# Gathered attention biases, key and query parts written straight to their partitions, 8 weight buffers, norm chunks one group ahead, 55 activation tiles

## Chip, cores and metric

The kernel runs on one core of a Trainium2 chip. The metric is the device time of one execution in microseconds (us), taken as the median of several runs; lower is better. TensorE (PE) does the matmuls, VectorE (DVE), ScalarE (ACT) and GpSimd (POOL) the elementwise work, and SyncE (SP) issues the DMAs.

## What is computed

Two layers of a diffusion backbone over 256 latent and 256 context tokens of width 1024. Cut to what matters:

```python
for l in range(2):
    h, hc = ffn_half_step(h, ...ffn1), ffn_half_step(hc, ...ffn1)
    u, uc = modulate(rmsnorm(h, g_mix)), modulate(rmsnorm(hc, g_mix))
    nq, nk, nv, fu, wq, wk, wv, gl = split_projection(u @ w_in[l])      # context likewise
    a = neighbourhood_attention(nq, nk, nv, nk_c, nv_c, na_bias[l])     # 8 heads of 64
    f = fourier_mix(fu)
    w = window_gqa_attention(rope(wq), rope(wk), wv, wk_c, wv_c, sink)  # 8 query heads, 2 key heads
    h = h + gt2 * merge_branches(a, f, w, gl, w_br[l], w_out[l])
    h = ffn_half_step(h, ...ffn2)                # the context stream stops after layer 0
return rmsnorm(h, g_final)
```

`ffn_half_step` is RMSNorm, scale and shift, SwiGLU of inner width 2816, and a gated addition to `h`. In the neighbourhood attention a latent query of column c sees 16 columns around c in all four grid rows, with a bias from a table of 15 by 31 entries for each head, and all context keys.

## The kernel before

Activations lie feature by token: a tile `act` (or `tmp`) is 128 partitions by 512 tokens in fp32, and 66 such tiles form one pool (`N_ACT`). Every product is done in three matmuls (`mm3`, lines 286 to 291): a value x is split into a rounded part "hi" and a remainder "lo" (= x - hi), and hi*hi, hi*lo and lo*hi are added up in PSUM. So each weight tile and each activation is split by one ACT instruction (hi) and one subtraction (lo).

The order of the instructions is written out by hand (`manual_schedule`): each engine runs its instructions in the order in which the program emits them, and waits in that order. A tile taken from a pool whose previous holder still has readers makes the first writer wait for the last of them.

Weights (`Weights`, lines 43 to 100) come as 424 sub-tiles of 128x1024 (8 tiles of 128x128). SP loads them into `raw` (line 58), ACT writes `wh` (line 67), DVE writes `wl` (line 76; POOL during attention and in the first FFN's first groups). `wh` and `wl` share the pool `w` of 6 buffers. At the first tile of sub-tile n (`next`, line 90) the program emits `wh` up to sub-tile n+2, and at its middle `wl` up to n+2.

A norm (`Norm`) makes the input u of a stage in 16 steps: step t (`_step`, lines 196 to 215) scales one 128x256 piece of `h` on DVE (line 206), adds the shift on ACT and rounds (line 208), and the piece of step t-1 gets its "lo" on DVE (line 214). `chunks(k)` runs the steps up to t = k+1. In an FFN the function `first` (lines 521 to 545) calls it ahead of the matmuls of group k: 4 weight tiles of 12 matmuls on 256 columns, first for the 8 latent pieces, then for the 8 context pieces. Two groups use one sub-tile of weights.

The mixer (`mix`, lines 844 to 1055): the Fourier branch and values are projected first, then `attention` (lines 713 to 842) walks over blocks (head pair p, latent or context queries) in a software pipeline: scores on PE (lines 726 and 727), mask and maximum on DVE (line 733), exp on ACT (line 735), normalising on DVE (line 752), transposes on PE (line 757), the split of the transposed weights on ACT (line 759) and DVE (line 764), and values on PE (line 775). Between its steps `fill` emits pieces of the projections of later blocks by due times. When a projection is done, `plain` (line 886, neighbourhood heads) or `rope` (line 896, window heads) takes it out of PSUM. `rope` turns it first: 4 small DMAs (line 903) and 3 POOL operations (line 906). Both then write hi (ACT, lines 889 and 909) and lo (DVE, lines 891 and 911) as 128-partition tiles, and `stack` (line 870) builds the operands of the scores from them by DMA on SP (line 884): for a query two tiles holding [hi0; lo0] and [lo1; hi1] of the two heads on 64 partitions each (4 DMAs), for a key four tiles [hi0; hi0], [hi1; hi1], [lo0; lo0], [lo1; lo1] (8 DMAs). There are 5 keys and 8 queries in each layer. Layer 0 works on 512 query tokens, layer 1 on 256; keys have 512 in both.

The masks of the neighbourhood attention: `mix_loads` takes 8 tiles `nab` from the activation pool in each layer, clears their context half on POOL (line 444) and loads the first head pair; `na_bias_load` (line 694) issues 8 DMAs for each head pair, which read rows of 64 fp32 numbers from a padded table, and `na_bias` (line 711) adds a window mask on POOL, 4 operations for each head pair. `bias_ahead` (line 1003) does that for the next pair in mid-attention and issues the loads of the pair after it.

Of the kernel before, what the change touches and what calls it, by code (L numbers as in the profile page):

```python
# [27 lines left out]
BIAS_W = 2 * GRID_W - 1  # L28
# [6 lines left out]
N_ACT = 66  # L35
# [224 lines left out]
class Emit:  # L260
    def __init__(self, ctx, tc, d):
        self.tc, self.nc, self.d = tc, tc.nc, d
        pool = lambda name, bufs, **k: ctx.enter_context(tc.tile_pool(name=name, bufs=bufs, **k))
        self.const = pool("const", 1)
        self.act_p = pool("act", N_ACT)
        self.raw_p = pool("raw", 5)
        self.w_p = pool("w", 6)
        self.mod_p = pool("mod", 2)
        self.sm_p = pool("sm", 4)
        self.ps_p = pool("ps", 8, space=PSUM)  # L270
        self.W = Weights(self.nc, d["ws"], self.raw_p, self.w_p)
        self.mod = {}
# [90 lines left out]
    def setup(self):  # L363
# [56 lines left out]
        self.na_mask = c.tile([128, NLAT], F32, name="na_mask")  # L420
# [5 lines left out]
    def setup_mix(self):  # L426
        nc, d = self.nc, self.d
        nc.sync.dma_start(out=self.g_fin, in_=d["g_final"])
        nc.sync.dma_start(out=self.cos, in_=d["cos"])
        nc.sync.dma_start(out=self.sin, in_=d["sin"])  # L430
        nc.sync.dma_start(out=self.na_mask, in_=d["na_mask"])
        nc.sync.dma_start(out=self.wa_mask, in_=d["wa_mask"])
        nc.sync.dma_start(out=self.sink, in_=d["sink"].partition_broadcast(128))
        yield
        nc.gpsimd.tensor_scalar(out=self.nsink, in0=self.sink, scalar1=-1.0, scalar2=None, op0=ALU.mult)

    def mix_loads(self, l):

        self.raw_dft = [self.tmp() for _ in range(2)]
        self.nc.sync.dma_start(out=self.raw_dft[0], in_=self.d["dft_n"])  # L440
        self.nc.sync.dma_start(out=self.raw_dft[1][:, :256], in_=self.d["dft_d"])
        self.nab = [[self.tmp() for _ in range(4)] for _ in range(2)]
        for t in self.nab[0] + self.nab[1]:
            self.nc.gpsimd.memset(t[:, NLAT:], 0.0)  # L444
        self.na_bias_load(l, 0)

# [61 lines left out]
    def ffn(self, l, which, n, norm, nxt):  # L508
# [12 lines left out]
        def first(passes):  # L521
# [3 lines left out]
            for vs in passes:  # L525
                lo, hi = 256 * vs[0], 256 * (vs[-1] + 1)
                for k in range(KD):
                    norm.chunks(vs[0] * KD + k)
# [165 lines left out]
    def na_bias_load(self, l, p):  # L694


        nc = self.nc
        tab = self.d["na_bias"]
        for i in range(4):
            t4 = self.nab[p % 2][i][:, :NLAT].rearrange("p (r c) -> p r c", c=GRID_W)  # L700
            hp, qt = divmod(i, 2)
            for r2 in range(2):
                first = WIN_R - 1 - (2 * qt + r2)
                off = ((l * 8 + 2 * p + hp) * GRID_W * (2 * WIN_R - 1) + first) * BIAS_W + GRID_W - 1
                src = bass.AP(tensor=tab.tensor, offset=tab.offset + off,
                              ap=[[(2 * WIN_R - 1) * BIAS_W - 1, GRID_W], [BIAS_W, ROWS], [1, GRID_W]])
                nc.sync.dma_start(out=t4[r2 * 64:r2 * 64 + 64], in_=src)  # L707

    def na_bias(self, p):
        for t in self.nab[p % 2]:  # L710
            self.nc.gpsimd.tensor_tensor(out=t[:, :NLAT], in0=t[:, :NLAT], in1=self.na_mask, op=ALU.add)
# [132 lines left out]
    def mix(self, l, norm, nxt):  # L844
# [9 lines left out]
        self.na_bias(0)  # L854
        self.na_bias_load(l, 1)
# [14 lines left out]
        def stack(name, hi, lo, n):  # L870


            a, b = self.act(), self.act()
            x, y = slice(0, 64), slice(64, 128)
            if "q" in name[0]:
                moves = (a, x, hi, x), (a, y, lo, x), (b, x, lo, y), (b, y, hi, y)
                res[name] = a, b
            else:
                c, d = self.act(), self.act()
                moves = ((a, x, hi, x), (a, y, hi, x), (b, x, hi, y), (b, y, hi, y),  # L880
                         (c, x, lo, x), (c, y, lo, x), (d, x, lo, y), (d, y, lo, y))
                res[name] = a, b, c, d
            for t, i, s, j in moves:
                nc.sync.dma_start(out=t[i, :n].bitcast(F32), in_=s[j, :n].bitcast(F32))

        def plain(scale):
            def evac(name, ps, n):
                hi, lo = self.act(), self.act()
                nc.scalar.activation(out=hi[:, :n], in_=ps[:, :n], func=AF.Copy, scale=scale)
                yield  # L890
                nc.vector.scalar_tensor_tensor(out=lo[:, :n], in0=ps[:, :n], scalar=scale,
                                               in1=hi[:, :n].bitcast(F32), op0=ALU.mult, op1=ALU.subtract)
                stack(name, hi, lo, n)
            return evac

        def rope(scale):
            def evac(name, ps, n):
# [10 lines left out]
                hi, lo = self.act(), self.act()  # L908
                nc.scalar.activation(out=hi[:, :n], in_=t, func=AF.Copy, scale=scale)
                yield  # L910
                nc.vector.scalar_tensor_tensor(out=lo[:, :n], in0=t, scalar=scale, in1=hi[:, :n].bitcast(F32),
                                               op0=ALU.mult, op1=ALU.subtract)
                stack(name, hi, lo, n)
# [89 lines left out]
        def bias_ahead(p):  # L1003
            self.na_bias(p)
            if p < 3:
                self.na_bias_load(l, p + 1)

# [122 lines left out]
def constants():  # L1130
# [7 lines left out]
    c = np.arange(GRID_W)  # L1138
    start = np.clip(c - WIN_C // 2, 0, GRID_W - WIN_C)
    inside = (c[None] >= start[:, None]) & (c[None] < start[:, None] + WIN_C)  # L1140
    na = np.where(inside, 0.0, NEG).astype(f)
# [13 lines left out]
        "na_mask": np.tile(na, (2, ROWS)),  # L1155
# [6 lines left out]
def pack(inputs, order):  # L1162
# [13 lines left out]
    pad = GRID_W - WIN_C  # L1176
    t = np.pad(w["na_bias"], ((0, 0), (0, 0), (0, 0), (pad, pad)))
    a["na_bias"] = np.broadcast_to(t[:, :, None], t.shape[:2] + (GRID_W,) + t.shape[2:])
# [31 lines left out]
    "na_bias": (DEPTH, 8, GRID_W, 2 * WIN_R - 1, BIAS_W), "sink": (DEPTH, 4, 4), "ident": (128, 128),  # L1210
    "cos": (128, NLAT), "sin": (128, NLAT), "na_mask": (128, NLAT), "wa_mask": (128, 2, NT),
# [18 lines left out]
```

## Time and profile before

| | us |
|---|---|
| median of 3 runs | 2122.66 (2122.08 to 2125.06) |
| profiled execution, its own time | 2120.81 |
| its span, first to last instruction | 2119.0 |
| PE busy / share of span | 2050.9 / 97% |
| DVE busy / share | 1283.7 / 61% |
| ACT busy / share | 848.5 / 40% |
| POOL busy / share | 355.7 / 17% |

The profiled execution is one run of the same program with the profiler on; its time stands 1.85 us below the median of the plain runs and 1.8 us above its own span. A stage can be found in the trace by its lines: the span runs through the first FFN of layer 0 (0 to 420 us), its mixer (420 to 860), second FFN (860 to 1240), and the same three of layer 1 (from 1240, 1600 and 1905).

### The profile page before, as it was taken

What the parts mean: (1) busy time and instruction counts of PE and PEld (TensorE: products, weight loads), DVE (VectorE), ACT (ScalarE), POOL (GpSimd) and SP (SyncE); (2) the same over time, 40 slices, a digit from 0 to 9 for tenths busy, and PEclk for the clock granted to TensorE, in tenths of its full rate; (3) what the DMA queues carried; (4) which work ended last, traced back from release to release, by engine and by line L of the source; (5) the groups of instructions that cost most, each with busy time, mean ns of one, the idle gap of its engine ahead of it and who ended that gap; (6) DMA issues with size and microseconds to landing.
All of it is one profiled execution on the core that took longest, in us unless ns stands there. A gap on an engine that the chain in (4) does not pass through costs nothing. (4 is left out here: it accounts for less than half of the span.)

```text
span 2119.0 us, 29168 instructions
## 1 busy us (share of the span) xinstructions
PE 2050.9 (97%) x11193; PEld 1764.7 (83%) x11193; DVE 1283.7 (61%) x2035; ACT 848.5 (40%) x1362; POOL 355.7 (17%) x285
## 2 busy tenths in 40 slices
PE   7899999999999999999999989999999989999998
PEld 3688888878888888988888788888888878999998
DVE  6777776566675334687777465533336548566554
ACT  4422222345786222432222243222324458545443
POOL 4200000403441112300000220000012155330002
PEclk9999999999999999999999999999999999999999
DMA  7465566455532333466666545623344563554663
GB/s 271 139 199 182 196 199 212 124 152 144 136 85 73 100 92 98 150 186 193 199 189 200 186 143 186 199 90 100 99 112 145 145 177 110 160 179 153 186 181 109
DMA packets 119412, 327.05 MB, mean 154 GB/s; under 512 B 30692, under 2 KB 35940, under 8 KB 119272
## 3 DMA queue, kind: packets, MB, share of 16 engines
q1 hardware_dynamic: 119272, 325.18, 50.3%
q8 instruction: 88, 1.44, 0.3%
q14 instruction: 52, 0.43, 0.1%
HBM read 305.99 MB, written 1.05 MB: 145 GB/s over the span
## 5 line engine op out<-in xcount | busy, mean ns | idle before, releaser
L290 PE MATMUL ps<-act,wh 128*128 128x512 f32 (+1 forms) x3227 | 1120.9, 347 | 24.1 <-DVE act L229 13.6
L289 PE MATMUL ps<-act,wh 128*128 128x512 f32 (+1 forms) x3227 | 1121.3, 347 | 3.4 <-ACT act L298 1.9
L291 PE MATMUL ps<-act,wl 128*128 128x512 f32 (+1 forms) x3227 | 1118.9, 347 | 1.8 <-DVE wl L76 1.8
L67 ACT ACTIVATE wh<-raw 128x1024 fp32r<-128x1024 f32 x424 | 447.4, 1056 | 707.8 <-PE ps L290 573.7
L290 PEld LDWEIGHTS ps<-act,wh 128*128 128x128 f32 x3227 | 613.2, 190 | 101.8 <-DVE act L229 14.8
L289 PEld LDWEIGHTS ps<-act,wh 128*128 128x128 f32 x3227 | 613.1, 190 | 78.9 <-ACT act L298 2.5
L291 PEld LDWEIGHTS ps<-act,wl 128*128 128x128 f32 x3227 | 613.1, 190 | 77.9 <-DVE wl L76 2.9
L76 DVE TENSOR_TENSOR wl<-raw,wh 128x1024 fp32r<-128x1024 f32 x379 | 474.6, 1254 | 273.6 <-ACT wh L67 273.0
L311 DVE CUSTOM_DVE_ANT_0 dump<-ada,silu_row 128x1024 bf16<-128x1024 f32 x224 | 273.3, 1220 | 13.9 <-DMA ada<-in_w_ada 11.5
L298 ACT ACTIVATE act<-tmp 128x512 fp32r<-128x512 f32 (+1 forms) x122 | 66.9, 566 | 275.2 <-DVE tmp L516 261.8
L471 DVE SCALAR_TENSOR_TENSOR h<-ps,mod,h 128x256 f32<-128x256 f32 x136 | 61.7, 480 | 150.8 <-PE ps L291 150.8
L76 POOL TENSOR_TENSOR wl<-raw,wh 128x1024 fp32r<-128x1024 f32 x45 | 110.7, 2461 | 222.9 <-ACT wh L67 199.7
L454 POOL TENSOR_TENSOR tmp<-h 128x512 f32<-128x512 f32 (+1 forms) x7 | 11.6, 1661 | 782.3 <-DVE h L471 639.8
L516 DVE TENSOR_TENSOR tmp<-tmp,ps 128x512 f32<-128x512 f32 (+1 forms) x88 | 54.6, 621 | 112.1 <-PE ps L291 107.5
L299 DVE TENSOR_TENSOR act<-tmp,act 128x512 fp32r<-128x512 f32 (+1 forms) x122 | 74.3, 625 | 62.2 <-ACT act L298 62.2
L764 DVE TENSOR_TENSOR act<-ps,act 128x512 fp32r<-128x512 f32 x80 | 54.8, 685 | 35.8 <-ACT act L759 27.6
L735 ACT ACTIVATE tmp<-tmp,sm 128x512 f32<-128x512 f32 (+1 forms) x96 | 62.2, 648 | 32.8 <-DVE sm L733 31.5
L775 PE MATMUL ps<-act 128*128 128x256 f32 x320 | 63.0, 309 | 12.4 <-DVE act L764 11.2
L460 POOL TENSOR_TENSOR tmp<-h 128x256 f32<-128x256 f32 (+1 forms) x44 | 51.7, 1174 | 117.8 <-DVE h L471 112.9
L759 ACT ACTIVATE act<-ps 128x512 fp32r<-128x512 f32 x80 | 47.5, 593 | 39.9 <-PE ps L757 34.5
L444 POOL MEMSET tmp<- 128x256 f32 x16 | 4.8, 312 | 348.6 <-PE ps L291 347.9
L775 PEld LDWEIGHTS ps<-act 128*128 128x128 f32 x320 | 44.8, 189 | 17.5 <-DVE act L764 15.0
(110 smaller groups left out, 1372.8 us busy)
## 6 DMA issues: line engine op xcount, KB each, us to landing
raw<-in_ws SPq DMA_DIRECT2D x424, 512.0 KB, 3.7
ada<-in_w_ada SPq DMA_DIRECT2D x128, 512.0 KB, 3.9
act<-act SPq DMA_DIRECT2D x112, 128.0 KB, 2.3
tmp<-in_w_ada_sc SPq DMA_DIRECT2D x16, 256.0 KB, 5.2
tmp<-in_w_ada SPq DMA_DIRECT2D x16, 256.0 KB, 6.0
tmp<-in_na_bias SPq DMA_DIRECT2D x64, 64.0 KB, 2.7
h<-in_h SPq DMA_DIRECT2D x8, 256.0 KB, 5.2
act<-act SPq DMA_DIRECT2D x32, 64.0 KB, 2.0
```

The costliest lines, as they stand in the source:

```text
L67: self.nc.scalar.activation(out=wh, in_=self.raw[i], func=AF.Copy)
L76: self.lo_engine.tensor_tensor(out=wl, in0=self.raw.pop(i), in1=self.hi[i].bitcast(F32), op=ALU.subtract)
L289: mm(ps, lhsT=w[0], rhs=x[0], start=start, stop=False)
L290: mm(ps, lhsT=w[0], rhs=x[1], start=False, stop=False)
L291: mm(ps, lhsT=w[1], rhs=x[0], start=False, stop=stop)
L298: nc.scalar.activation(out=hi, in_=src, func=AF.Copy)
L299: nc.vector.tensor_tensor(out=lo, in0=src, in1=hi.bitcast(F32), op=ALU.subtract)
L311: self.nc.vector.tensor_tensor_reduce(out=self.dump[:, ks], in0=w, in1=self.silu_row[:, v, ks], scale=1.0, scalar=m if half else 0.0, op0= ...
L471: self.nc.vector.scalar_tensor_tensor(out=h, in0=ps, scalar=self.mod[l, g][:, v, j:j + 1], in1=h, op0=ALU.mult, op1=ALU.add)
L735: nc.scalar.activation(out=e[:, :nk], in_=e[:, :nk], func=AF.Exp, scale=-1.0, bias=nm, accum_out=b["sum"][:, i:i + 1])
L764: nc.vector.tensor_tensor(out=t[1], in0=ps, in1=t[0].bitcast(F32), op=ALU.subtract)
L775: nc.tensor.matmul(b["ps"][hp][:, :256], lhsT=v, rhs=t[j][:, cs], start=c == 0 and j == 0, stop=c == n - 1 and j == 1)
```

## The change

- `na_bias` is prepared outside the program as full 256x256 masked tables, so that one DMA of 512 KB loads a head pair; the POOL additions, the mask tile and its load are gone. `nab` becomes two tiles of 128 x 4 x 512 for the whole run, cleared once in `setup`, and both are loaded in `mix_loads`.
- `stack` reads the projection itself and writes the parts to the partitions where they belong: two ACT and two DVE instructions on 64 partitions each. A query needs no DMA any more, a key 4. The 128-partition hi and lo tiles are gone.
- The `w` pool has 8 buffers; `ahead` is as it was.
- In `first`, `chunks` is called for one group further (not in the very first FFN).
- `N_ACT` is 55.

```diff
-N_ACT = 66
+N_ACT = 55
-        self.w_p = pool("w", 6)
+        self.w_p = pool("w", 8)
@@ setup
-        self.na_mask = c.tile([128, NLAT], F32, name="na_mask")
+        self.nab = [c.tile([128, 4, NT], F32, name=f"nab{i}") for i in range(2)]
+        for t in self.nab:
+            nc.gpsimd.memset(t[:, :, NLAT:], 0.0)
@@ mix_loads
-        self.nab = [[self.tmp() for _ in range(4)] for _ in range(2)]
-        for t in self.nab[0] + self.nab[1]:
-            self.nc.gpsimd.memset(t[:, NLAT:], 0.0)
         self.na_bias_load(l, 0)
+        self.na_bias_load(l, 1)
@@ ffn, first
-                    norm.chunks(vs[0] * KD + k)
+                    norm.chunks(vs[0] * KD + k + (not norm.ready))
@@ na_bias_load (its loops of 8 DMAs, and na_bias, are gone)
+        self.nc.sync.dma_start(out=self.nab[p % 2][:, :, :NLAT], in_=self.d["na_bias"][l, p])
@@ mix
-        self.na_bias(0)
-        self.na_bias_load(l, 1)
-        def stack(name, hi, lo, n):
-            a, b = self.act(), self.act()
+        def stack(name, src, scale, n):
             x, y = slice(0, 64), slice(64, 128)
+            a, b = self.act()[:, :n], self.act()[:, :n]
             if "q" in name[0]:
-                moves = (a, x, hi, x), (a, y, lo, x), (b, x, lo, y), (b, y, hi, y)
+                parts = (a, x, a, y, x), (b, y, b, x, y)
+                moves = ()
             else:
-                c, d = self.act(), self.act()
-                moves = ((a, x, hi, x), (a, y, hi, x), (b, x, hi, y), (b, y, hi, y),
-                         (c, x, lo, x), (c, y, lo, x), (d, x, lo, y), (d, y, lo, y))
-            for t, i, s, j in moves:
-                nc.sync.dma_start(out=t[i, :n].bitcast(F32), in_=s[j, :n].bitcast(F32))
+                c, d = self.act()[:, :n], self.act()[:, :n]
+                parts = (a, x, c, x, x), (b, y, d, y, y)
+                moves = (a, x, y), (b, y, x), (c, x, y), (d, y, x)
+            for hi, i, _, _, s in parts:
+                nc.scalar.activation(out=hi[i], in_=src[s], func=AF.Copy, scale=scale)
+            yield
+            for hi, i, lo, j, s in parts:
+                nc.vector.scalar_tensor_tensor(out=lo[j], in0=src[s], scalar=scale, in1=hi[i].bitcast(F32),
+                                               op0=ALU.mult, op1=ALU.subtract)
+            for t, i, j in moves:
+                nc.sync.dma_start(out=t[j].bitcast(F32), in_=t[i].bitcast(F32))
+            res[name] = (a, b) if "q" in name[0] else (a, b, c, d)
@@ plain and rope: both now end in stack(name, ps or t, scale, n)
@@ na_block
-                            after=(lambda: bias_ahead(p + 1)) if lat and p < 3 else None,
-                            mask=self.nab[p % 2] if lat else [zero] * 4,
+                            after=(lambda: self.na_bias_load(l, p + 2)) if lat and p < 2 else None,
+                            mask=[self.nab[p % 2][:, i, :] for i in range(4)] if lat else [zero] * 4,
```

## Rows read from the trace of the kernel before

**Rows 1.** The page, busy us, share of the span and instructions of each engine

```profile
PE 2050.9 (97%) x11193; PEld 1764.7 (83%) x11193; DVE 1283.7 (61%) x2035; ACT 848.5 (40%) x1362; POOL 355.7 (17%) x285
```

**Rows 2.** Stretches: length, busy PE, PEld, DVE, ACT, POOL, PE clock, DMA share, GB/s

```profile
500.00:680.00 180.00, 174.78 (x971) 147.99 (x970) 124.13 (x308) 134.12 (x325) 73.57 (x60) 1.00 0.41 109
1240.00:1280.00 40.00, 32.26 (x246) 30.34 (x245) 26.38 (x46) 19.64 (x30) 1.23 (x2) 1.00 0.44 134
1600.00:1640.00 40.00, 37.44 (x239) 33.32 (x238) 28.78 (x51) 21.05 (x33) 8.48 (x11) 1.00 0.55 159
1660.00:1820.00 160.00, 146.36 (x1017) 133.96 (x1016) 91.94 (x189) 104.24 (x226) 79.02 (x56) 0.99 0.54 143
```

**Rows 3.** ACT, then DVE, in time, start of layer 1's first FFN

```profile
1254.17 1.06 ACT L67 ACTIVATE wh<-raw 128x1024 fp32r<-128x1024 f32 x1 [1.09 <-PE ps L290]
1258.52 1.06 ACT L67 ACTIVATE wh<-raw 128x1024 fp32r<-128x1024 f32 x1 [1.09 <-PE ps L290]
...
1255.27 1.22 DVE L76 TENSOR_TENSOR wl<-raw,wh 128x1024 fp32r<-128x1024 f32 x1 [1.55 <-ACT wh L67]
1257.59 0.47 DVE L214 SCALAR_TENSOR_TENSOR act<-tmp,mod,act 128x256 fp32r<-128x256 f32 x1
```

**Rows 4.** ACT in time, start of layer 0's second FFN

```profile
884.61 1.06 ACT L67 ACTIVATE wh<-raw 128x1024 fp32r<-128x1024 f32 x1
887.78 1.04 ACT L67 ACTIVATE wh<-raw 128x1024 fp32r<-128x1024 f32 x1
```

**Rows 5.** Waits of the whole span: who, for whom, us, times, longest

```profile
PE ps L290 <- DVE act L214: 7.5, 6, 1.4
```

**Rows 6.** Waits, 1660 to 1820 us, PE and ACT

```profile
PE ps L775 <- DVE act L764: 9.0, 7, 2.9
...
ACT wh L67 <- PE ps L290: 16.0, 8, 4.4
```

**Rows 7.** Waits, 1698 to 1728 us

```profile
DVE act L891 <- DMA act<-act: 7.5, 1, 7.5
DVE act L764 <- DMA act<-act: 7.4, 1, 7.4
...
PE ps L932 <- ACT tmp L928: 2.2, 1, 2.2
...
PE ps L757 <- ACT tmp L900: 1.4, 1, 1.4
```

**Rows 8.** SP in time, 1698 to 1717 us: start, us, instructions merged

```profile
1697.46 5.33 SPq L707 DMA_DIRECT2D tmp<-in_na_bias  x8
1706.67 7.82 SPq L884 DMA_DIRECT2D act<-act  x12
```

**Rows 9.** By line: duration ns min/median/max, first and last start, forms

```profile
L891 DVE SCALAR_TENSOR_TENSOR act<-ps,act x16: 411/684/693, 478.0 to 1707.6; 128x512 fp32r<-128x512 f32 x12, 128x256 fp32r<-128x256 f32 x4
L911 DVE SCALAR_TENSOR_TENSOR act<-tmp,act x10: 462/692/2126, 569.6 to 1773.5; 128x512 fp32r<-128x512 f32 x6, 128x256 fp32r<-128x256 f32 x4
L889 ACT ACTIVATE act<-ps x16: 364/578/600, 477.3 to 1700.8; 128x512 fp32r<-128x512 f32 x12, 128x256 fp32r<-128x256 f32 x4
L781 ACT ACTIVATE tmp<-ps x96: 361/379/387, 523.1 to 1814.0; 64x256 f32<-64x256 f32 x96
```

**Rows 10.** Waits of PE, 500 to 680 us

```profile
PE ps L726 <- DMA act<-act: 1.8, 1, 1.8
```

**Rows 11.** DVE in time at the start of layer 1's mixer

```profile
1614.82 0.83 DVE L214 SCALAR_TENSOR_TENSOR act<-tmp,mod,act 128x256 fp32r<-128x256 f32 x1 [0.19 <-ACT act L208]
1618.22 2.88 DVE L76 TENSOR_TENSOR wl<-raw,wh 128x1024 fp32r<-128x1024 f32 x2
```

**Rows 12.** Memsets by line (as rows 9); POOL and ACT in time at the start

```profile
L444 POOL MEMSET tmp<- x16: 312/312/313, 232.2 to 1433.3; 128x256 f32 x16
...
26.59 3.38 POOL L221 TENSOR_TENSOR tmp<-h,tmp 128x512 f32<-128x512 f32 x2
...
30.09 1.09 ACT L227 ACTIVATE act<-tmp,mod,mod 128x256 fp32r<-128x256 f32 x2 [4.00 <-DVE mod L318]
```

More of the change, by code (lines that the diff above doesn't have):

```diff
@@ L27 @@
 WINDOW = 128
-BIAS_W = 2 * GRID_W - 1
 O_NA_Q, O_NA_K, O_NA_V, O_FN, O_WA_Q, O_WA_K, O_WA_V, O_GATE = (
@@ L430, in setup_mix @@
         nc.sync.dma_start(out=self.sin, in_=d["sin"])
-        nc.sync.dma_start(out=self.na_mask, in_=d["na_mask"])
         nc.sync.dma_start(out=self.wa_mask, in_=d["wa_mask"])
@@ L694, in na_bias_load @@
     def na_bias_load(self, l, p):
[L697 to L711, printed above, removed]
+        self.nc.sync.dma_start(out=self.nab[p % 2][:, :, :NLAT], in_=self.d["na_bias"][l, p])
     def attention(self, makers, fill):
@@ L868, in project @@
                 yield
-        def stack(name, hi, lo, n):
-            a, b = self.act(), self.act()
+        def stack(name, src, scale, n):
             x, y = slice(0, 64), slice(64, 128)
+            a, b = self.act()[:, :n], self.act()[:, :n]
             if "q" in name[0]:
-                moves = (a, x, hi, x), (a, y, lo, x), (b, x, lo, y), (b, y, hi, y)
-                res[name] = a, b
-            else:
-                c, d = self.act(), self.act()
-                moves = ((a, x, hi, x), (a, y, hi, x), (b, x, hi, y), (b, y, hi, y),
-                         (c, x, lo, x), (c, y, lo, x), (d, x, lo, y), (d, y, lo, y))
-                res[name] = a, b, c, d
-            for t, i, s, j in moves:
-                nc.sync.dma_start(out=t[i, :n].bitcast(F32), in_=s[j, :n].bitcast(F32))
-        def plain(scale):
[L887 to L894, printed above, removed]
+                parts = (a, x, a, y, x), (b, y, b, x, y)
+                moves = ()
+            else:
+                c, d = self.act()[:, :n], self.act()[:, :n]
[10 more added lines that the diff above has]
+            res[name] = (a, b) if "q" in name[0] else (a, b, c, d)
+        def plain(scale):
+            return lambda name, ps, n: stack(name, ps[:, :n], scale, n)
         def rope(scale):
@@ L907, in evac @@
                 yield 1
[L908 to L913, printed above, removed]
+                yield from stack(name, t, scale, n)
             return evac
@@ L1001, in mix @@
         zero = self.wa_mask[:, 0, NLAT:]
[L1003 to L1006, printed above, removed]
         def split_out(o, p):
@@ L1137, in constants @@
     cos, sin = np.cos(ang).T, np.sin(ang).T
[L1138 to L1141, printed above, removed]
     band = np.where(np.abs(t[:, None] - t[None]) <= WINDOW, 0.0, NEG).astype(f).reshape(2, 128, NLAT)
@@ L1154, in constants @@
         "sin": np.concatenate([-sin, sin] * 2, 0),
-        "na_mask": np.tile(na, (2, ROWS)),
         "wa_mask": wa,
@@ L1175, in pack @@
     a["w_ada_sc"] = w["w_ada"][0, :, D:2 * D].reshape(KD, 128, 2, 512).transpose(2, 0, 1, 3)
-    pad = GRID_W - WIN_C
-    t = np.pad(w["na_bias"], ((0, 0), (0, 0), (0, 0), (pad, pad)))
-    a["na_bias"] = np.broadcast_to(t[:, :, None], t.shape[:2] + (GRID_W,) + t.shape[2:])
+    c, t = np.arange(GRID_W), np.arange(NLAT)
+    start = np.clip(c - WIN_C // 2, 0, GRID_W - WIN_C)
+    inside = (c[None] >= start[:, None]) & (c[None] < start[:, None] + WIN_C)
+    row, col = t // GRID_W, t % GRID_W
+    dr = row[None] - row[:, None] + WIN_R - 1
+    dc = np.clip(col[None] - col[:, None], 1 - WIN_C, WIN_C - 1) + WIN_C - 1
+    b = np.full((DEPTH, 8, NLAT, NLAT), NEG, np.float32)
+    inside = np.tile(inside, (ROWS, ROWS))
+    b[:, :, inside] = w["na_bias"][:, :, dr[inside], dc[inside]]
+    a["na_bias"] = b.reshape(DEPTH, 4, 2, 2, 128, NLAT).transpose(0, 1, 4, 2, 3, 5).reshape(DEPTH, 4, 128, 4, NLAT)
     s = w["wa_sink"]
@@ L1209 @@
     "c": (128, KD, 2), "b_ada": (128, DEPTH, 9, KD), "gains": (128, DEPTH, 3, 8), "g_final": (128, 8),
-    "na_bias": (DEPTH, 8, GRID_W, 2 * WIN_R - 1, BIAS_W), "sink": (DEPTH, 4, 4), "ident": (128, 128),
-    "cos": (128, NLAT), "sin": (128, NLAT), "na_mask": (128, NLAT), "wa_mask": (128, 2, NT),
+    "na_bias": (DEPTH, 4, 128, 4, NLAT), "sink": (DEPTH, 4, 4), "ident": (128, 128),
+    "cos": (128, NLAT), "sin": (128, NLAT), "wa_mask": (128, 2, NT),
     "dft_n": (128, 2 * NLAT), "dft_d": (128, 256),
```

## The prediction

> **What bounds the kernel now.** I read the page first: PE is busy for 97% of the span [rows 1], so an engine with less work helps only where PE waits for it. No matmul is added, taken away or reordered here, so the whole effect must come out of PE's idle time, some 68 us (2119.0 less 2050.9). The first 80 us, where much of that lies, are touched only by two memsets. I then read the table of stretches for idle time elsewhere: 7.7 us at the start of layer 1's first FFN (40 less 32.26), 5.2 us in layer 0's attention, 2.6 us where layer 1's mixer starts, and 13.6 us in layer 1's attention, the largest [rows 2]. Last I read, for those stretches, who ended the waits, and the instructions in order of time.
>
> At the FFN start PE waits six times, 7.5 us in all, for the "lo" part of a norm chunk, DVE L214 [rows 5]. The time order shows a loop: ACT's conversion `wh` waits 1.09 us for PE to leave a weight buffer, DVE's `wl` waits for that `wh`, and the chunk that PE needs next stands behind `wl` on DVE; one turn takes 1258.52 - 1254.17 = 4.35 us [rows 3]. The same work in layer 0's second FFN, where ACT does not wait for PE, turns in 887.78 - 884.61 = 3.17 us [rows 4].
>
> In layer 1's attention the largest waits of PE (2.9, 2.2 and 1.4 us) lie within 12 us of each other [rows 6, 7]. Just ahead DVE stood 7.5 and 7.4 us until a DMA `act<-act` had read a tile: the pool gave its slot to a new writer, and the move that still had to read the old hi or lo tile was queued on SP [rows 7]. SP was busy with 8 bias loads (5.33 us) and 12 moves in a row (7.82 us) [rows 8]. So the bound there is SP's issue time, through the tile pool.
>
> **The change part by part.** The sum is made against the profiled execution (2120.81 us); the median of the runs shown, 2122.66, is 1.85 us higher, and I carry the difference over to it.
>
> (1) 8 weight buffers and chunks one group ahead. The buffers take away ACT's wait for PE, the earlier chunk takes L214 out of the group that needs it; either cuts the loop. I take the turn of rows 4 for that of rows 3: 6 waits x 1.18 us = 7.1 us gained. Next late is DVE and ACT's own rhythm, which is why the turn stays at 3.17. Bounds: 3.5 us if only half of the turns shorten, 8.5 us if the group in hand also covers some of that rhythm in both FFNs. The chunk's DVE and ACT instructions only move; what they pass on DVE is one `wl` (1.22 us, rows 3), which has a sub-tile in hand.
>
> (2) The bias loads become one DMA instead of 8 for each head pair, queries lose their 4 moves and keys 4 of 8: in the stretch of rows 8 seven of the eight bias issues and more than half of the moves go, some 9 of 13 us. The hi and lo tiles whose slots DVE waited for exist no more. I count the three waits of PE (2.9 + 2.2 + 1.4) as gone: 6.5 us. Bounds: 3.5 us (half), 13.6 us (all idle time of the stretch).
>
> (3) Against that each of the 26 stacks gets one more ACT and one more DVE instruction. That a half of the partitions is no cheaper is shown by L781, 379 ns on 64 partitions against 364 for the same 256 columns on 128 [rows 9]. So a stack costs up to 0.58 us more on ACT and 0.69 on DVE (512 columns), 0.36 and 0.41 to 0.46 on 256. All of DVE's would be 13 x 0.69 in layer 0 and 5 x 0.69 + 8 x 0.44 in layer 1, 16.0 us. PE does wait for DVE there: 9.0 us in 7 times for L764 [rows 6], of which 2.9 belong to (2), the rest mostly where L764 stands behind L911. I charge layer 1's five window stacks in full (0.69 + 4 x 0.46 = 2.5 us) and 1.0 us in layer 0, where ACT is busy for 75% and DVE for 69% of the stretch [rows 2]: a loss of 3.5 us. Bounds: 0 and 16.0; less than nothing isn't excluded by POOL's bias additions going, but (5) carries that.
>
> (4) ACT waits 16.0 us of layer 1's attention for a weight buffer [rows 6], with splits and exponentials queued behind. With 8 buffers that goes. What it gives PE beyond (2) isn't shown: between 0 and the 7.1 us of idle time then left there; I take 2.0, near the lower end, since most of these waits end while PE has work.
>
> (5) POOL's additions of the mask go (32 in all). Where a mixer starts they ran beside the norm's chunks and DVE was slower: L214 took 0.83 us against 0.47, two `wl` 2.88 against 2 x 1.22 [rows 3, 11]. I take 1.0 us in layer 1 and 0.5 in layer 0; bounds 0 and 2.6 (the idle time of rows 2) for each.
>
> (6) The first scores of layer 0 waited 1.8 us for a move [rows 10]. This is a key's, and 4 of its 8 issues (7.82 / 12 = 0.65 us each, rows 8) go, 2.6 us. So 1.8 us gained, at least 0.
>
> (7) Two memsets of 4 x 256 columns now stand on POOL at the start, 2 x 4 x 0.312 = 2.5 us, between `wl` and the first L221. The first L221 would end 2.5 us after 28.3, and ACT, which waits for DVE until 30.09, would be 0.7 us late [rows 12]; later DVE waits there can swallow it. Loss 0.5 us, bounds 0 and 2.5.
>
> (8) 55 tiles cost nothing by my count: walking through the old program in order, the pool's peak is 65 tiles alive in layer 1's attention; 8 `nab` and a stack's hi and lo leave 55. It fits, with no more slack than now; the rival below prices the case that it doesn't do.
>
> Sum: 7.1 + 6.5 - 3.5 + 2.0 + 1.5 + 1.8 - 0.5 = 14.9 us. The profiled execution would be 2105.9 us, the median 2107.8.
>
> Part (3) meets a rule that speaks against the change. The rows show it first: L891, with one operand in PSUM, stays between 411 and 693 ns, while L911, with both in SBUF, ranges from 462 to 2126 [rows 9]. The Trainium skill, "SBUF — State Buffer", section "Who interferes with whom", says that a DVE instruction with two SBUF inputs contends with a GpSimd instruction that reads SBUF, and that the loser waits for the whole of the other. By that rule ten of the 26 new DVE instructions, those of `rope`, are exposed to POOL's weight splits and the other sixteen are not. The trace agrees. What it would give as a result is the third rival.
>
> **The rivals.** First, the attention stays bound by ACT and DVE, and their added work eats what SP gives back: two thirds of the 16.0 us of (3), 10.3 us, against (2), (4) and (6), 10.3 us. What is left is (1), (5) and (7), 8.1 us: 2114.6 us. For it speaks that the chain there runs to and fro between DVE and ACT after 1760; against it, that the three largest waits have another cause.
>
> Second, more is freed: all of PE's idle time in layer 1's attention (13.6), 8.5 in (1), 1.8 in (6), 2.5 in (5), less 0.5: 25.9 us, 2096.8 us. For it speaks that waits follow on each other there; against it (3).
>
> Third, slower: the ten new DVE instructions of `rope` stand behind POOL's weight splits as the worst L911 did, 10 x 2.126 = 21.3 us, and the sixteen of `plain` lie on PE's path in full (12 x 0.69 + 4 x 0.41 = 9.9). 31.2 us against gains of 18.4 (all but (3)): 12.8 us slower, 2135.5. It decides from 18.4 us on, 0.71 for each stack. Against it: only one of ten L911 took 2.1 us, and PE has idle time and slack in layer 0.
>
> Fourth, the change doesn't free the queue because 55 tiles are too few: new writers wait for the readers of the last ones, and (2) and (6) come to nothing. 14.9 - 8.3 = 6.6 us gained, 2116.1. For it speaks that at the peak no slot is spare, as before; against it, that the late readers were DMAs, and those are mostly gone.
>
> **How the numbers follow.** Chances: forecast 0.60, first rival 0.17, second 0.11, fourth 0.08, third 0.04. The time predicted is 2107.8. The range reaches from a little below the second rival to a little above the fourth, 2095 to 2117; outside it lie the third, a part of the fourth and tails. A measurement of this kernel tells about 0.2% from no change, so faster means below 2118.4 and slower above 2126.9. Faster: all but the third rival, some of the fourth and tails of the first, 0.89. Same: 0.06. Slower: 0.05.
>
> **What would show it.** For (1): no wait of PE for L214 at the start of layer 1's first FFN, ACT's `wh` there without a wait for PE, turns of 3.2 us or less. For (2): no wait of DVE for `act<-act`, SP with one bias issue at a time, layer 1's attention idle for some 8 us instead of 13.6. For (3): PE's waits for L764 in the window blocks as long as before or longer, and a spread of the new L911 up to 2 us. For (7): the first L221 2.5 us later and PE caught up by 80 us. The prediction is wrong if the attention's idle time stays at 13 us with SP free, which would point to (3), or if waits for tile slots appear with readers other than DMAs.

## The result, and the profile after

The changed kernel takes 2133.5 us (median of 4 runs, 2131.27 to 2136.95) against 2122.4 for the kernel before: a ratio of 1.0054, 95% interval 1.0035 to 1.0073. It is slower by 0.54%, where 2107.8 was forecast (range 2095 to 2117). The profiled execution took 2136.95 us, with a span of 2134.1.

The page of the changed kernel gives busy us, share of the span and instructions of each engine [rows 1]:

```profile
PE 2066.2 (97%) x11193; PEld 1778.1 (83%) x11193; DVE 1299.9 (61%) x2061; ACT 856.3 (40%) x1388; POOL 341.5 (16%) x239
```

The number of matmuls is the same, and yet PE is busy for 15 us more: some of them ran slower. (3.5 of the 15 us lie in the first 100 us, 82.22 busy at a granted clock of 0.86 against 78.74 at 0.91; both kernels get 261 matmuls done there, so that part costs no time.) The stretches of rows 2 tell where (length, then busy PE, PEld, DVE, ACT, POOL, granted PE clock, DMA share, GB/s):

```profile
500.00:680.00 180.00, 165.86 (x901) 139.62 (x900) 125.68 (x305) 130.82 (x317) 61.62 (x46) 0.96 0.25 72
1240.00:1280.00 40.00, 39.58 (x321) 38.38 (x320) 29.94 (x52) 20.45 (x32) 4.91 (x6) 1.00 0.54 161
1600.00:1640.00 40.00, 38.14 (x266) 34.90 (x265) 28.84 (x44) 18.29 (x27) 11.83 (x10) 1.00 0.56 161
1660.00:1820.00 160.00, 142.83 (x906) 128.04 (x905) 100.45 (x200) 102.13 (x219) 64.25 (x41) 0.95 0.35 101
```

Start of layer 1's first FFN: idle time 7.74 us before, 0.42 now. Layer 0's attention: 5.2 before, 14.1 now, at a granted clock of 0.96 instead of 1.00. Layer 1's attention: 13.6 before, 17.2 now, at 0.95 instead of 0.99. So the gain of the first term is there, and the two attentions together lose more than it.

For whom PE waits in layer 0's attention (500 to 680 us; us, times, longest), first before the change:

```profile
PE ps L775 <- DVE act L764: 2.2, 7, 0.3
```

then in the changed kernel:

```profile
PE ps L758 <- DVE act L747: 10.5, 12, 2.6
PE ps L758 <- ACT act L742: 2.6, 3, 1.6
```

and in layer 1's (1660 to 1820 us) [rows 6, 7]:

```profile
PE ps L758 <- DVE act L747: 12.4, 7, 4.0
PE ps L907 <- ACT tmp L903: 2.3, 1, 2.3
PE ps L740 <- ACT tmp L880: 1.8, 1, 1.8
```

L747 is the DVE split that was L764, L758 the values matmul that was L775. PE's waits for the split grew from 2.2 us to 10.5 in layer 0 and from 9.0 to 12.4 in layer 1. Of the three waits that the forecast gave to SP's queue the first, 2.9 us for L764, is gone. The other two stand under new line numbers: L932's for L928 (2.2 us) is now L907's for L903 (2.3), and L757's for L900 (1.4) is L740's for L880 (1.8). What stands ahead of L747 is shown by the durations of the new subtraction, L867 (ns min/median/max) [rows 9]:

```profile
L867 DVE SCALAR_TENSOR_TENSOR act<-ps,act x32: 417/683/696, 474.1 to 1710.6; 64x512 fp32r<-64x512 f32 x24, 64x256 fp32r<-64x256 f32 x8
L867 DVE SCALAR_TENSOR_TENSOR act<-tmp,act x20: 419/685/2739, 567.8 to 1787.9; 64x512 fp32r<-64x512 f32 x12, 64x256 fp32r<-64x256 f32 x8
```

The 32 of the neighbourhood heads (`plain`), which read PSUM, never take more than 0.70 us. Of the 20 of the window heads (`rope`), which have both operands in SBUF, the longest takes 2.74. One pair of them in order of time, DVE first:

```profile
576.25 3.44 DVE L867 SCALAR_TENSOR_TENSOR act<-tmp,act 64x512 fp32r<-64x512 f32 x2 [1.72 <-ACT act L864]
579.72 0.42 DVE L716 CUSTOM_DVE_ANT_0 tmp<-ps,wa_mask 128x256 f32<-128x256 f32 x1
...
580.15 0.67 DVE L747 TENSOR_TENSOR act<-ps,act 128x512 fp32r<-128x512 f32 x1
```

then POOL and PE of the same kernel and time:

```profile
576.27 2.88 POOL L75 TENSOR_TENSOR wl<-raw,wh 128x1024 fp32r<-128x1024 f32 x1
...
578.10 0.38 PE L758 MATMUL ps<-act 128*128 128x256 f32 x1 [1.59 <-ACT act L742]
580.88 1.01 PE L758 MATMUL ps<-act 128*128 128x256 f32 x3 [2.39 <-DVE act L747]
581.68 0.63 PE L288 MATMUL ps<-act,wh 128*128 128x512 f32 x1
```

The first L867 takes its usual 0.69 us. POOL's weight split starts 0.02 us after it, and the second L867 stands until the split has ended: the two together take 3.44 us, 2.07 more than two medians. L747, queued behind, starts at 580.15, and PE waits 2.39 us for it. The windows around it (as above) show what follows:

```profile
570.00:576.00 6.00, 5.57 (x32) 4.80 (x33) 4.46 (x13) 5.64 (x14) 3.37 (x5) 1.00 0.45 123
576.00:581.00 5.00, 1.01 (x7) 0.58 (x5) 4.68 (x8) 2.78 (x8) 3.14 (x2) 0.76 0.00 0
581.00:586.00 5.00, 5.00 (x18) 4.12 (x19) 2.04 (x6) 1.84 (x6) 0.00 (x0) 0.56 0.08 22
586.00:590.00 4.00, 4.00 (x24) 3.45 (x24) 3.73 (x10) 2.77 (x8) 2.22 (x3) 1.00 0.44 137
```

After 4 us of 5 without work PE runs at a granted clock of 0.56, close to the 1.2 GHz level, through the next window, and at 2.4 GHz again after it. One late DVE instruction costs PE its wait, and then a few microseconds at half speed in which it is "busy". This happens at three of layer 0's four window queries: the pairs at 594.62 and 618.74 us take 3.45 and 3.46 us, with a granted clock of 0.66 from 599 to 604 and from 623 to 628 us.

The same place before the change, DVE and POOL:

```profile
576.98 0.69 DVE L911 SCALAR_TENSOR_TENSOR act<-tmp,act 128x512 fp32r<-128x512 f32 x1 [1.18 <-ACT act L909]
...
577.06 2.84 POOL L76 TENSOR_TENSOR wl<-raw,wh 128x1024 fp32r<-128x1024 f32 x1
```

The one subtraction of the stack went ahead of POOL's split by 0.08 us, and so it did at the next two queries (590.54 ahead of 590.63, 610.22 ahead of 610.30). POOL paid: its split took 2.84 instead of 2.4. A second instruction behind the first was all that it took to have one on the wrong side.

There is a second new wait, in layer 1. DVE's waits (1660 to 1820 us), and the longest of them in order of time:

```profile
DVE tmp L716 <- PE ps L758: 8.7, 4, 5.4
DVE act L747 <- PE ps L709: 6.2, 1, 6.2
```

```profile
1719.62 0.68 DVE L747 TENSOR_TENSOR act<-ps,act 128x512 fp32r<-128x512 f32 x1
1725.66 0.69 DVE L716 CUSTOM_DVE_ANT_0 tmp<-ps,nab 128x512 f32<-128x512 f32 x1 [5.36 <-PE ps L758]
```

L716 writes a fresh score tile and reads nothing that L758 makes. So it waits for a reader of the tile that held its slot: the pool of 55 has none to give. (The profile doesn't name slots; `w7_57` below, with two tiles more, doesn't have this wait.) Before, DVE waited there for moves `act<-act` [rows 7]; those waits are gone, and matmuls have taken their place as the last readers.

### The profile page after: what moved, and what is told of

Read it like the earlier page. It is cut to its first block, busy times and chain, and to the rows that moved or that the text cites. A ratio compares the mean times of both kernels' runs of the same rounds, so it can differ in the third digit from the quotient of the medians.

```text
span 2134.1 us, 28828 instructions
## 1 busy us (share of the span) xinstructions
PE 2066.2 (97%) x11193; PEld 1778.1 (83%) x11193; DVE 1299.9 (61%) x2061; ACT 856.3 (40%) x1388; POOL 341.5 (16%) x239
## 5 line engine op out<-in xcount | busy, mean ns | idle before, releaser
L289 PE MATMUL ps<-act,wh 128*128 128x512 f32 (+1 forms) x3227 | 1124.6, 348 | 12.7 <-DVE act L228 10.4
L66 ACT ACTIVATE wh<-raw 128x1024 fp32r<-128x1024 f32 x424 | 436.4, 1050 | 317.1 <-PE ps L289 281.6
L513 ACT ACTIVATE tmp<-ps 128x512 f32<-128x512 f32 (+1 forms) x88 | 47.8, 543 | 124.3 <-PE ps L290 123.6
L758 PE MATMUL ps<-act 128*128 128x256 f32 x320 | 68.0, 322 | 26.3 <-DVE act L747 23.0
L458 POOL TENSOR_TENSOR tmp<-h 128x256 f32<-128x256 f32 (+1 forms) x44 | 64.1, 1458 | 107.7 <-DVE h L469 92.3
L747 DVE TENSOR_TENSOR act<-ps,act 128x512 fp32r<-128x512 f32 x80 | 55.0, 687 | 36.3 <-ACT act L742 23.3
L758 PEld LDWEIGHTS ps<-act 128*128 128x128 f32 x320 | 47.7, 199 | 33.5 <-DVE act L747 28.6
```

Of the source, the lines that this page charges most:

```text
L66: self.nc.scalar.activation(out=wh, in_=self.raw[i], func=AF.Copy)
L289: mm(ps, lhsT=w[0], rhs=x[1], start=False, stop=False)
L458: nc.gpsimd.tensor_tensor(out=sq, in0=h, in1=h, op=ALU.mult)
L758: nc.tensor.matmul(b["ps"][hp][:, :256], lhsT=v, rhs=t[j][:, cs], start=c == 0 and j == 0, stop=c == n - 1 and j == 1)
```

## The experiments

All times are medians beside runs of the kernel before on the same chip; the ratio is to those, with its 95% interval. Differences below some 4 us (0.2%) are not told from none. The kernel before took 2122.8 us beside `w7_57`, `rope_moves`, `rope_pool` and `rope_oneinput`, 2122.0 beside `w7_55`, `rope_psum`, `plain_moves` and `split_pool`, and 2123.7 beside the other four. Where two kernels of different groups are compared, the difference of their distances from the kernel before stands in brackets. The diffs show the deciding lines only.

| kernel | us | ratio |
|---|---|---|
| w7_57 | 2124.3 | 1.0011 (1.0002 to 1.0020) |
| w7_55 | 2135.3 | 1.0066 (1.0051 to 1.0081) |
| rope_moves | 2113.8 | 0.9957 (0.9942 to 0.9972) |
| rope_pool | 2115.8 | 0.9965 (0.9954 to 0.9976) |
| rope_oneinput | 2130.2 | 1.0042 (1.0026 to 1.0059) |
| rope_psum | 2112.1 | 0.9958 (0.9942 to 0.9975) |
| plain_moves | 2128.2 | 1.0031 (1.0018 to 1.0044) |
| split_pool | 2103.4 | 0.9919 (0.9904 to 0.9934) |
| s_noahead | 2109.2 | 0.9935 (0.9920 to 0.9950) |
| s_w6_59 | 2101.3 | 0.9901 (0.9886 to 0.9915) |
| s_biasold | 2107.7 | 0.9930 (0.9915 to 0.9944) |
| before_rope | 2146.7 | 1.0113 (1.0093 to 1.0132) |

**w7_57 and w7_55: tiles or buffers.** Two kernels below need two more tiles, so their control has one weight buffer less.

```diff
-N_ACT = 55
+N_ACT = 57
-        self.w_p = pool("w", 8)
+        self.w_p = pool("w", 7)
```

> The changed kernel with 7 weight buffers and 57 tiles; its time is the control for the two kernels that need two more tiles. Lock theory (the second DVE subtraction of a window stack, L867, stands behind POOL's weight split for some 2.7 us, PE waits for the L747 behind it): nothing of that is touched, 2129 to 2137 us, L867's longest near 2.7 us. Tile rival (55 tiles are too few): with two more tiles most of the loss goes, 2110 to 2120. Buffer rival (the two extra buffers move POOL's splits onto the stacks): some us faster.

2124.3 us, 9.2 (9.6) less than the changed kernel, between the two expectations. L867 still takes up to 2736 ns. So something costs time beside the lock, the tiles or the buffer. w7_55 has the buffers of this control and the tiles of the changed kernel:

```diff
-        self.w_p = pool("w", 8)
+        self.w_p = pool("w", 7)
```

> The changed kernel with 7 weight buffers and 55 tiles, to tell what made the control with 7 buffers and 57 tiles 9 us faster than the changed kernel. If it was the two tiles (new writers wait for slots): 2130 to 2136 us, as the changed kernel. If it was the buffer (with 8 the splits of ACT and POOL fall elsewhere): 2121 to 2127. The start of layer 1's first FFN keeps its gain in both.

2135.3 us: it is the two tiles, 11.0 us (11.8), and the eighth buffer does nothing that shows (2133.5 with it). DVE waits for L758 and L709 (6.3 and 6.2 us in layer 1) stand in w7_55 as in the changed kernel, and neither is among the waits of w7_57. The granted clock of 1700 to 1810 us is 0.92 in the changed kernel and 0.97 in w7_57.

**rope_psum: the operand alone.** The same instructions, with one operand in PSUM:

```diff
-                nc.vector.scalar_tensor_tensor(out=lo[j], in0=src[s], scalar=scale, in1=hi[i].bitcast(F32),
+                nc.vector.scalar_tensor_tensor(out=lo[j], in0=(src if ps is None else ps)[s], scalar=scale, in1=hi[i].bitcast(F32),
-                yield from stack(name, t, scale, n)
+                yield from stack(name, t, scale, n, ps[:, :n])
```

> 7 buffers, 57 tiles, new stacks everywhere; the two subtractions of each window stack read the projection in PSUM instead of the rotated tile in SBUF, so they have one operand in PSUM and one in SBUF as the neighbourhood stacks have (the remainder of the window queries and keys is that of other numbers then). Same number of instructions and elements as the control. Lock theory: each stays under 0.75 us even beside POOL's split, PE's waits for L747 shrink, 2110 to 2119 us against the control's 2124. If the number of instructions is the cause: 2122 to 2127. Against both: the projection's bank is held some 10 us longer, which would show as waits of PE for a bank.

2112.1 us, 12.2 (11.4) less than its control, with as many instructions. The remainder is taken from the projection before it is turned, so this kernel leaves out the rotation there: it is a test and not a way out. All of its L867, by duration:

```profile
L867 DVE SCALAR_TENSOR_TENSOR act<-ps,act x52: 417/683/696, 473.4 to 1762.6; 64x512 fp32r<-64x512 f32 x36, 64x256 fp32r<-64x256 f32 x16
```

and the pair that answers to the one shown above, DVE and POOL:

```profile
574.99 1.41 DVE L867 SCALAR_TENSOR_TENSOR act<-ps,act 64x512 fp32r<-64x512 f32 x2 [1.25 <-ACT act L864]
...
575.07 2.37 POOL L75 TENSOR_TENSOR wl<-raw,wh 128x1024 fp32r<-128x1024 f32 x1
```

The second subtraction runs in the middle of POOL's split, and neither loses a nanosecond that shows: 1.41 us for two, 2.37 for the split. PE is busy for 94.0 of the 100 us from 560 on at a granted clock of 1.00, against 88.1 at 0.95 in the control. This settles the lock between DVE and POOL, and that the number of instructions is not the cause in layer 0. The rule quoted in the prediction (the Trainium skill, "SBUF — State Buffer", section "Who interferes with whom") says of two SBUF inputs just this, and the rows agree.

**rope_oneinput: one SBUF operand.**

```diff
+                if one:
+                    nc.vector.tensor_scalar(out=lo[j], in0=hi[i].bitcast(F32), scalar1=scale, scalar2=None, op0=ALU.mult)
+                    continue
```

> The changed kernel (8 buffers, 55 tiles) where the two subtractions of each window stack are a multiplication of the hi part by the scale: as many DVE instructions on as many elements, with one SBUF operand instead of two; it leaves out the remainder of the window queries and keys. Lock theory (it needs two operands in SBUF): these instructions stay under 1 us, PE's waits for L747 fall to under 10 us, 2107 to 2119 us. If the lock takes any SBUF operand, or if the number of instructions or the queue is the cause: 2128 to 2136, nearly as the changed kernel.

2130.2 us, so the second expectation came true: an operation with a single SBUF operand waits as well. Its durations:

```profile
L868 DVE TENSOR_SCALAR act<-act x20: 286/422/2276, 567.7 to 1780.1; 64x512 fp32r<-64x512 f32 x12, 64x256 fp32r<-64x256 f32 x8
```

and one pair in order of time, DVE, then POOL's split:

```profile
591.27 0.42 DVE L868 TENSOR_SCALAR act<-act 64x512 fp32r<-64x512 f32 x1 [0.65 <-ACT act L864]
591.92 2.28 DVE L868 TENSOR_SCALAR act<-act 64x512 fp32r<-64x512 f32 x1 [0.23 <-ACT act L864]
...
591.35 2.56 POOL L75 TENSOR_TENSOR wl<-raw,wh 128x1024 fp32r<-128x1024 f32 x1
```

Free, this form takes 0.42 us on 64x512 where the subtraction takes 0.69; beside the split it takes 2.28. It was a poor choice for my question, as "takes one operand" also changed how fast it ran. The same section of the Trainium skill lists `tensor_scalar` among the operations that have a mode which takes the shared ports; these rows agree with that.

**rope_moves and rope_pool: two ways out.** On the control's 57 tiles. The first gives the window heads their old stack back:

```diff
-                yield from stack(name, t, scale, n)
+                hi = full.bitcast(F32R)
+                nc.scalar.activation(out=hi[:, :n], in_=t, func=AF.Copy, scale=scale)
+                yield
+                nc.vector.scalar_tensor_tensor(out=t, in0=t, scalar=scale, in1=full[:, :n],
+                                               op0=ALU.mult, op1=ALU.subtract)
+                move(name, full, t, n)
```

> The changed kernel (7 weight buffers, 57 tiles) with the stacks of the window heads as before: one ACT and one DVE instruction on 128 partitions, then 4 or 8 DMA moves; the neighbourhood stacks stay new. Lock theory: PE's waits for L747 in the two attentions fall from some 23 us to under 10 and the time by 14 to 25 us against its control, 2107 to 2119 us. Instruction rival (it is the number of ACT and DVE instructions, whichever stack they belong to): 10 of the 26 stacks are undone, so a third of the loss at most returns, 2122 to 2130. Queue rival (SP's issues and bias loads): more moves on SP, no faster than the control.

The second keeps the new stack and gives its subtractions to POOL:

```diff
+                if pool:
+                    nc.gpsimd.tensor_tensor(out=lo[j], in0=src[s], in1=hi[i].bitcast(F32), op=ALU.subtract)
+                    continue
-                yield from stack(name, t, scale, n)
+                yield from stack(name, t, 1.0, n, True)
```

> The changed kernel (7 weight buffers, 57 tiles) with the two subtractions of each window stack on POOL instead of DVE (ACT scales when it copies the projection). POOL cannot run them beside its own weight split, so DVE never stands behind one for them. Lock theory: 2107 to 2119 us, PE's waits for L747 under 10 us in both attentions together. Instruction rival: DVE loses 20 of its 52 stack instructions, some 2124 to 2130. Against both: POOL's own subtractions and the splits behind them come later, which would show as waits of PE for weights.

2113.8 and 2115.8 us, 10.5 and 8.5 less than the control, both within what the lock theory gave. But they gain in different places. In layer 0 (560 to 660 us) PE is busy for 96.8 us with the moves and 91.1 with POOL, against 88.1 in the control; in layer 1 (1700 to 1810 us) for 94.2 and 100.3, against 96.5. In layer 1 its waits for L747 are 12.8 us with the moves, no better than the control's 10.4, and 6.0 with POOL. The totals of both layers, 15.3 and 11.0 us, didn't fall under 10 as expected; with the moves the gain was all in layer 0, with POOL it was in both.

**plain_moves: the other 16 stacks undone.** The neighbourhood heads get the old stack, the window heads keep the new one.

```diff
-            return lambda name, ps, n: stack(name, ps[:, :n], scale, n)
+            def evac(name, ps, n):
+                hi, lo = self.act(), self.act()
+                nc.scalar.activation(out=hi[:, :n], in_=ps[:, :n], func=AF.Copy, scale=scale)
+                yield
+                nc.vector.scalar_tensor_tensor(out=lo[:, :n], in0=ps[:, :n], scalar=scale,
+                                               in1=hi[:, :n].bitcast(F32), op0=ALU.mult, op1=ALU.subtract)
+                move(name, hi, lo, n)
```

> 7 buffers, 57 tiles; the stacks of the neighbourhood heads as before (one ACT and one DVE instruction on 128 partitions, then 4 or 8 moves), those of the window heads new. Lock theory: the 16 plain stacks have one operand in PSUM and cost PE nothing, so the time stays within 4 us of the control, 2120 to 2128. Instruction rival: 16 of 26 stacks are undone, 2113 to 2119. Queue rival (the moves were what hurt): slower than the control, since SP gets its moves back and two more tiles are in use.

2128.2 us, 3.9 (4.6) more than the control: about the limit of what can be told. The instruction rival expected 2113 to 2119, and undoing 16 of the 26 stacks gains nothing. The old stacks hold two more tiles, which may hide a gain, so this alone doesn't decide; together with rope_psum, which is faster with as many instructions, it does. Whether their moves cost something on SP, as the queue rival had it, can't be told from so small a difference.

**before_rope: that one part alone.** The kernel before, with its 66 tiles and 6 buffers, and only `rope` ending in the new stack (`parts_stack` is `stack` of the changed kernel).

```diff
-                hi, lo = self.act(), self.act()
-                nc.scalar.activation(out=hi[:, :n], in_=t, func=AF.Copy, scale=scale)
-                yield
-                nc.vector.scalar_tensor_tensor(out=lo[:, :n], in0=t, scalar=scale, in1=hi[:, :n].bitcast(F32),
-                                               op0=ALU.mult, op1=ALU.subtract)
-                stack(name, hi, lo, n)
+                yield from parts_stack(name, t, scale, n)
```

> The kernel before with one part of the change alone: the window heads' stacks written straight to their partitions (two ACT and two DVE instructions, 4 moves for the key, none for the queries), 66 tiles, 6 buffers, all else as before. Lock theory: the second subtraction stands behind POOL's split, and as its tiles and SP's queue don't bind here, slower by 6 to 14 us: 2128 to 2136. If the loss of the changed kernel came from the tiles alone: 2116 to 2123, as the moves that go give some of SP's time back.

2146.7 us, 23.0 more than the kernel before and 11 beyond my upper end. The subtraction's durations:

```profile
L902 DVE SCALAR_TENSOR_TENSOR act<-tmp,act x20: 418/687/2741, 569.9 to 1799.2; 64x512 fp32r<-64x512 f32 x12, 64x256 fp32r<-64x256 f32 x8
```

and the windows of 100 us of layer 0's attention and 110 us of layer 1's:

```profile
560.00:660.00 100.00, 87.22 (x463) 72.78 (x462) 73.15 (x174) 73.04 (x182) 34.88 (x30) 0.93 0.18 55
1700.00:1810.00 110.00, 91.25 (x575) 82.50 (x574) 64.39 (x130) 66.48 (x148) 61.61 (x47) 0.91 0.50 131
```

In layer 0 it loses what the changed kernel loses there (86.75 busy at 0.93). In layer 1 SP's moves and the lock come together: DVE's waits for `act<-act` (7.8 and 7.3 us) are there, as before the change (7.5 and 7.4), and PE's waits for the split L764 are 15.0 us instead of 9.0. Why this part alone costs more than the expectation allowed isn't shown beyond that.

**split_pool and three variations of it.** The window stacks with moves in layer 0 and on POOL in layer 1, 57 tiles and 7 buffers:

```diff
+                if l:
+                    yield from stack(name, t, 1.0, n, True)
+                    return
+                hi = full.bitcast(F32R)
...
```

> A version meant to beat both: 7 buffers, 57 tiles, neighbourhood stacks new; window stacks in layer 0 with one ACT and one DVE instruction and moves, in layer 1 with two ACT instructions and two subtractions on POOL. In layer 0 PE was busy for 96.8 us of 560 to 660 us with the moves and 91.1 with POOL's subtractions, in layer 1 for 94.2 and 100.3 of 1700 to 1810, so by the lock theory the gains add up: 2104 to 2111 us. If the two layers' gains aren't separate (what comes early in layer 1 only waits later): 2112 to 2116.

2103.4 us, faster than the kernel before by 0.8%, and 0.6 below what was expected if the gains add up. They do (10.5 and 8.5 apart, 20.9 (20.1) together), with each layer in the form that was better there. The stretches of layer 0 and layer 1:

```profile
560.00:660.00 100.00, 96.70 (x564) 82.05 (x564) 78.54 (x202) 83.70 (x218) 39.55 (x35) 1.00 0.34 90
...
1700.00:1810.00 110.00, 98.37 (x750) 91.56 (x751) 72.06 (x147) 87.22 (x200) 66.04 (x51) 1.00 0.35 102
```

> The kernel split_pool (2103.4 us) with the norm's chunks again called with the group that needs them, 7 weight buffers. If either part of the first term cuts the loop at the start of layer 1's first FFN (as the prediction says): 2102 to 2106 us and no wait of PE for L213 there. If the earlier chunks do it: 2108 to 2112, with the 7.5 us of waits for L213 back.

```diff
-                    norm.chunks(vs[0] * KD + k + (not norm.ready))
+                    norm.chunks(vs[0] * KD + k)
```

2109.2 us, 5.8 (4.1) more. Of the waits for L213 there one of 1.3 us comes back, not 7.5. In the 40 us from 1240 on PE is idle for 2.3 us, against 0.4 in split_pool and 7.7 before: the buffers alone take most of it away and the chunks the rest. The rest of the difference I can't place.

> The kernel split_pool with 6 weight buffers, as before the change, and 59 tiles in place of 57. If the earlier chunks alone cut the loop and tile slots still bound layer 1's attention: 2096 to 2102 us. If 57 tiles are enough already and the buffers are not needed: 2102 to 2105. If the buffers are needed: ACT's waits for PE return and 2106 to 2112.

```diff
-N_ACT = 57
+N_ACT = 59
-        self.w_p = pool("w", 7)
+        self.w_p = pool("w", 6)
```

2101.3 us, the fastest of all, though 2.1 us (3.8) from split_pool is not told from none. PE is idle for 0.4 us from 1240 to 1280: with the chunks ahead, the extra buffers aren't needed. In layer 1's attention PE's waits for L747 fall from 7.1 to 2.8 us.

> The kernel split_pool with the biases as before: 8 small DMAs for each head pair from the padded table, and the window mask added on POOL, 4 operations for each pair; nab stays two fixed tiles. The prediction gave (2) the issue time of SP and (5) 1.5 us for POOL's additions. If these carry: 2106 to 2113 us, with SP's bias issues ahead of the moves in layer 1's attention. If SP's time was bounded by the pool alone and the additions are hidden: 2102 to 2105.

```diff
-        self.nc.sync.dma_start(out=self.nab[p % 2][:, :, :NLAT], in_=self.d["na_bias"][l, p])
+                nc.sync.dma_start(out=t4[r2 * 64:r2 * 64 + 64], in_=src)
...
+            self.nc.gpsimd.tensor_tensor(out=t, in0=t, in1=self.na_mask, op=ALU.add)
```

2107.7 us, 4.3 (2.5) more: what the biases are worth is not told from none. PE's wait for `wl` where layer 1's mixer starts, 2.1 us before and 1.3 in the changed kernel, is 2.1 again.

## Why the prediction was wrong

The parts as measured (in brackets by the distances from the kernel before): the window subtractions 12.2 us lost (11.4; w7_57 to rope_psum), two tiles 11.0 lost (11.8; w7_55 to w7_57), chunks 5.8 (4.1), biases 4.3 (2.5) and neighbourhood stacks 3.9 (4.6) gained. That is 9.2 us lost (12.0), against 11.1 measured for the whole. The parts come from different bases, the gains are small beside what can be told, and the buffers' own part of (1) is not among them, so this agreement is only a rough one.

- (1) held: forecast 7.1, bounds 3.5 to 8.5. Idle time at the FFN start fell by 7.3 us, there is no wait of PE for L213 from 1240 to 1280 us, and `wh` turns in 1260.88 - 1257.83 = 3.05 us. That either part cuts the loop is borne out: of 7.7 us idle 2.3 are left with 7 buffers alone (s_noahead) and 0.4 with the chunks alone (s_w6_59).
- (2) held in part. Waits for `act<-act` are gone, and the bias load is one issue of 0.60 us, as the prediction asked to see. But of the three waits that it counted as gone, 6.5 us, only the first (2.9) was SP's. The other two stand in the changed kernel (2.3 and 1.8 us) and, at 1.4 to 1.5 us each, in w7_57, rope_pool, split_pool and s_w6_59: why ACT is late there is open. Layer 1's attention is idle for 17 us with the bias issues and most moves gone from SP, and waits for slots have readers other than DMAs: the two signs that the prediction named for its being wrong. The moves of the window queries belong to (2) as well, and removing them was no gain: rope_psum without them takes 2112.1 us, rope_moves with them 2113.8.
- (5) and (6) held. PE's idle time at the start of each mixer (420 to 500 and 1600 to 1660 us) fell from 2.6 us to 1.9, where 0.5 and 1.0 were forecast, and the wait of 1.8 us for a key's move is gone.
- (3) is the step that failed. It charged 2.5 us in layer 1 and 1.0 in layer 0 on the ground of instruction lengths. The 12.2 us (11.4) measured for the window stacks are inside its bounds of 0 to 16.0, but they lay mostly in layer 0 (PE idle from 500 to 680 us for 12.8 us in w7_57 and 6.7 in rope_psum; from 1660 to 1820 us for 13.5 and 13.2), for the reason of the third rival: the lock. I set that rival at 0.04 because only one of ten L911 had taken 2.1 us. What I didn't look at was why the other nine had not: three of layer 0's four query stacks had gone ahead of POOL's split by 0.08 to 0.09 us. I had read their durations [rows 9], not their starts beside POOL's. With a margin of 0.08 us a second instruction of 0.69 had to fall behind. The clock that PE loses after such a wait was in no term at all.
- (4) did not come: ACT's waits for PE in layer 1's attention went from 16.0 to 1.9 us, and PE gained nothing that shows. In s_w6_59, with 6 buffers, 8.8 us of them are back, and it is the fastest of all.
- (7) was small, as said: the two memsets take 1.84 us, the first L220 starts at 28.71 instead of 26.59, and ACT's L226 at 30.27 instead of 30.09.
- (8) failed too: nothing forecast, 11.0 us (11.8) measured. "No more slack than now" was wrong by its own count: 66 tiles against a peak of 65 left one slot to spare, 55 against 55 leave none. That it "fits" says nothing of when the last reader of a slot is done. The fourth rival had this mechanism, but priced it only at the gains it would undo (8.3 us), not at waits of its own, and argued that the late readers had been DMAs; matmuls took their place.
- The third rival's 2135.5 lies close to the 2133.5 measured, but not by its own sum. Three of its ten instructions took 2.7 us (another three of the 20 took 0.80 to 0.88), the sixteen plain ones cost nothing that shows, and the rest of the loss came with PE's lower clock and the tiles, which it didn't have.
- The first rival took the added ACT and DVE time itself for the bound. plain_moves and rope_psum speak against it: with all 26 added pairs in place rope_psum is faster than the kernel before by 0.4%. (Two thirds of 16.0 are 10.7 us and not 10.3; that moves its 2114.6 by 0.4.)

## What to carry to other kernels

Before an instruction is split in two, look in the order of time at what GpSimd does around it, and by how much it escapes today; a median says nothing when the margin is 0.08 us. A subtraction that has to run beside GpSimd work should read one operand in PSUM if its value lies there, go to GpSimd itself, or stay a single instruction. A pool that just fits can have a price: ask who the last reader of each slot is, and leave some spare. Two tiles were worth 11 us here.

## What the runs showed of the hardware

- Two SBUF operands on DVE beside a GpSimd split of two SBUF operands: 2.72 to 2.74 us instead of 0.69; with one operand in PSUM 0.69. `tensor_scalar` with one SBUF operand: up to 2.28 instead of 0.42 (rope_oneinput). Kernels before and after have this in the normalising too (L752 and L735, median 0.48 us, longest 2.25 and 2.62), where it wasn't tried to remove it.
- The one that starts first runs at its length and the other stands for it: GpSimd's split takes 2.81 to 2.88 us when the subtraction was ahead, 2.4 without.
- On GpSimd the subtraction takes 0.73 us for 64x256 and 1.27 for 64x512 (rope_pool, minimum and median).
- PE's granted clock after some 4 us with little work was 0.56 for about 5 us. In rope_psum, without these waits, it is 1.00 from 560 to 660 us; that the clock follows the waits was read from such windows and not tried by itself.
